# First head's K, V and q on GpSimd's queue, another order of the rooms of the second attention, and index sums over two score pieces

## The chip, the cores and the metric

The kernel runs on one core of a Trainium2 chip. The metric is the device time of one execution in microseconds. Engines are named as in the profile: PE is TensorE, DVE VectorE, ACT ScalarE, POOL GpSimd, SP SyncE. A `q` behind an engine's name (ACTq, SPq) marks what its instruction queue does without keeping the engine busy, the issue of a DMA above all.

## The reference

Two layers over 2048 tokens of width 1024 in float32. Layer 0 is a forgetting attention of 8 heads, layer 1 a sparse attention in which a light indexer picks at most 256 keys for each query. Cut to the lines that matter here:

```
for i in range(DEPTH):
    x = _layer_norm(DN_ALPHA * x + mixers[i % N_MIXERS](x), ln_g[i], ln_b[i], LN_EPS)
# layer 1, one block of 128 queries
isc = jnp.einsum('bqhd,bsd->bqhs', qi_b, ki) * di ** -0.5
isc = jnp.einsum('bqhs,bqh->bqs', jax.nn.relu(isc), wi_b)
isc = jnp.where(kpos <= qpos, isc, -jnp.inf)
_, idx = lax.top_k(isc, k_sel)
logits = jnp.einsum('bqhc,bqkc->bhqk', qf_b, sel) * dh ** -0.5
p = jax.nn.softmax(logits, axis=-1)
...
return (jax.nn.silu(gate) * o) @ w_out
```

So the index of a query block is a sum over 8 index heads of relu(score) times a weight. The kernel does not gather keys; it finds the threshold of the top 256, writes a mask, and runs a masked dense attention.

## The kernel before

Nearly every product is made of three float16 products (a high and a low half of each operand, `mm3`, lines 319 to 321), added in PSUM. PE has the most work of all engines. The program runs through these stages, with the times that they take in the profile: the projections of layer 0 (0 to 680 us), attention of layer 0 (680 to 1160), its output projection (1160 to 1430), the projections of layer 1 with the index woven in (1430 to 2030), attention of layer 1 (2030 to 2515), and its output projection (to the end).

**Rooms.** A stage takes its buffers from a pool. `PHASE` says how many rooms a tag has, `SIZE` how large they are, `ORDER` in which order the tags lie in the memory. The pools of successive stages lie over each other, so a tile of a new stage waits until the old tiles under it have been used for the last time (`reuse_waits="tile"`). For attention of layer 1 the old tiles are the eight `KV` (layer 1's input, two for each chunk of 512 tokens, used by the gate projection to its very end), and behind them the rooms of the index. `TURNED` names the rooms that transposed probabilities take in turn.

**Attention.** For each head `load_kv` loads K (two pieces, each in two DMAs in layer 1, `kr` and `kn`, line 994) and V (two pieces, line 1005); `load_chunk` loads the queries of a chunk (line 1013). Later heads' loads stand in SP's queue, head 0's K and V in ACT's. For a row of 128 queries PE makes the scores in pieces of 512 columns; DVE moves each to the row `PR` with bias or mask and takes the largest (line 1077, and 1090 scales it); ACT takes the exponential (1091) and copies it to float16 (`PP`, 1099); POOL subtracts to have the low half (`sub`, line 325); SP turns two rows by one transposing DMA (1104) into `PX`, `PT` or `PU`; PE multiplies by V (`O <- PX,V`).

**Index.** `scores` makes relu(q k) for each index head in pieces of at most 512 columns: two matmuls to a PSUM tile (1502, 1503), ACT's relu to a tile `SC` (1505, three rooms), and DVE's multiply and add to the row `x` in `GA`, `GB` or `GC` (1508 for the first head, 1510 for the others). The threshold search (`select`) is woven between, and so are the last projection tiles: `rest` in `dsa_jobs` goes tile by tile through 6 to 21, each over chunks 0 to 3. Tiles 14 to 21 are the gate, which is written to `scr_g` (372) and loaded again at `gate` (1029). Masks are made on DVE (1671) and stored from POOL's queue (1672).

**Order.** The code is written in one stream. A scheduler with its own timeline of costs (`schedule_with_timeline_sim`) then picks the order of the instructions of each engine, so any change of rooms or sizes can move instructions elsewhere. Each engine works through its own list in order. A DMA in SP's or ACT's list shares one of eight semaphores with other DMAs of these two and waits until the one before it on that semaphore has landed; DMAs of POOL's list have eight of their own. A waiting DMA holds up all that is behind it in the same list.

Of the kernel before, what the change touches and what calls it, by code (L numbers as in the profile page):

```python
# [15 lines left out]
F16 = mybir.dt.float16  # L16
OP = mybir.AluOpType
AF = mybir.ActivationFunctionType
# [29 lines left out]
BUFS = {"W": 6, "E": 8, "RW": 3, "QS": 2, "SC": 3, "ty": 9, "tz": 4, "tb": 2, "mb": 2}  # L48
PHASE = ({"KV": 8}, {"K": 4, "V": 2, "PT": 1, "PU": 1, "PX": 1, "PR": 4, "PP": 3, "I": 1, "N": 3},
         {"K": 4, "V": 2, "PT": 1, "PU": 1, "PX": 1, "PR": 4, "PP": 3, "M": 1, "N": 3}, {"P": 8},  # L50
         {"A": 3, "X": 15}, {"P": 8}, {})
ORDER = ((), ("N", "I", "PR", "PT", "pad1", "PU", "K", "PP", "V", "PX"),
         ("N", "M", "PX", "PR", "K", "V", "PP", "pad2", "PT", "PU"), ("pad3", "P"), ("A", "X"), (),
         ("st", "GB", "u", "GA", "GC", "spare"))
SIZE = {"K": 2048, "V": 4096, "PT": 8192, "PU": 8192, "PX": 8192, "PR": 4096, "PP": 4096, "I": 128, "N": 256,
        "M": 2432, "pad1": 3200, "pad2": 896, "pad3": 4096, "P": 4096, "A": 4096, "X": 4096, "st": 4096,
        "u": 3584, "spare": 4096, "GA": 8448, "GB": 10752, "GC": 7936}
TURNED = ("PT", "PU", "PX")

PS_BUFS = {"S": 3, "T": 2, "U": 2, "O": 1}  # L60
UTAGS = "SUSUS"
# [16 lines left out]
FTAGS = "STUSTUS"  # L78
SCAN = 2

WOP = (((0, 1), (2, 3), (4, 5), (6, 7)), ((3, 4), (2, 5), (6, 7), (1, 0)))
OGS = (0, 1, 2, 3), (0, 1, 1, 1)
OGE = 3
AHEAD = 13
# [146 lines left out]
class Trunk:  # L231
# [748 lines left out]
    def load_kv(self, layer, h):  # L980
        nc = self.nc
        st = {"layer": layer}

        rooms = FIRSTK[layer] if h == 0 else (("K", 1024), ("K", 1024))
        st["k"] = []

        def key(s):
            while sum(n for _, n in rooms[:len(st["k"])]) < s + 1024:
                tag, n = rooms[len(st["k"])]
                a = sum(n for _, n in rooms[:len(st["k"])])  # L990
                to = self.t(tag, [128, 2, n], F16)
                for rows, name, r in ((slice(0, 32), "kr", 0), (slice(32, 128), "kn", h * 96)) if layer else (
                        (slice(0, 128), "k1", h * 128),):
                    (nc.sync if h else nc.scalar).dma_start(
                        to[rows], self.scr[name][r:r + rows.stop - rows.start, :, a:a + n])
                st["k"].append(to)
                for b in range(a, a + n, 512):
                    st[b] = to[:, :, b - a:b - a + 512]

        def value(s):  # L1000
            if s == 0:
                st["v"] = self.t("V", [128, NT, 2, 128], F16)
            t = s // 128
            v = self.scr["v2" if layer else "v1"][h]
            (nc.sync if h else nc.scalar).dma_start(st["v"][:, t:t + 8], v[:, t:t + 8])

        return st, [partial(f, s) for f in (key, value) for s in range(0, S, 1024)]

    def load_chunk(self, layer, h, c):
        nc = self.nc  # L1010
        cs = {"layer": layer, "h": h, "c": c, "l": self.sums[:, c, 4 * h:4 * h + 4], "halves": []}
        q, parts = self.pair(("SC" if layer else "RW") if (h, c) == (0, ORD[layer][0]) else "E")
        nc.sync.dma_start(q, self.scr["q2" if layer else "q1"][c, h * 128:(h + 1) * 128])
        cs["q"] = parts
        if layer:
            return cs
        if self.rel[0] != h:
            self.rel = h, [self.t("W", [128, 1024]) for _ in range(2)]
            for a, t in enumerate(self.rel[1]):
                nc.sync.dma_start(t, self.scr["rel"][h:h + 1, a * 1024:a * 1024 + 1024].to_broadcast([128, 1024]))  # L1020
        cs["rel"] = self.rel[1]
        return cs
# [26 lines left out]
    def qk_tile(self, cs, j, i):  # L1049

        nc = self.nc
        c = cs["c"]
        qt = 4 * c + j
        n = (qt + 1) * 128
        at = i * (c + 1) * 512 if c < MERGE else 0
        if at == 0:
            cs["row"] = self.t("PR", [128, S])
            if c < MERGE or i:
                cs["pair"] = self.t("PP", [128, 2 * S], F16)
        off = 2 * i * (n - 128) if c < MERGE else 0  # L1060
        row = cs["row"][:, at:at + n]
        pair = cs["pair"][:, off:off + 2 * n] if c < MERGE or i else None
        mn = None
        for a, b in self.cuts(n, 512):
            w = b - a
            sc = self.psum(QTAGS[self.unit_i % len(QTAGS)])
            self.unit_i += 1
            qh, ql = (t[:, j * 128:(j + 1) * 128] for t in cs["q"])
            kh, kl = (cs["kv"][a][:, x, :w] for x in range(2))
            self.mm3(sc[:, :w], qh, ql, kh, kl, True, True)  # L1070
            if cs["layer"] == 0 and b == n:
                nc.tensor.matmul(sc[:, n - 128 - a:n - a], self.eye, self.cmask, start=False, stop=True,
                                 skip_group_check=True)
            for lo, bias in self.biases(cs, qt, a, b):
                hi = lo + bias.shape[-1]
                m2 = self.tiny(1)
                nc.vector.tensor_tensor_reduce(out=row[:, lo:hi], in0=sc[:, lo - a:hi - a], in1=bias,  # L1077
                                               op0=OP.add, op1=OP.min, scale=-1.0, scalar=3e38 if mn is None else mn,
                                               accum_out=m2)
                mn = m2  # L1080
            if b < n:
                yield
        if i == 0:
            yield "turn"
            self.half_i += 1
            turned = self.t(TURNED[self.half_i % len(TURNED)], [128, 4 * qt + 6, 128], F16)
            cs["halves"].append({"cs": cs, "half": j // 2, "T": turned})
        up = self.tiny(1)
        per, neg = (self.scale(x, cs["layer"]) for x in ("per", "neg"))
        nc.vector.tensor_scalar(up, mn, per, SHIFT * float(np.log(2.0)), op0=OP.mult, op1=OP.add)  # L1090
        nc.scalar.activation(row, row, AF.Exp, bias=up, scale=neg, accum_out=cs["l"][:, j:j + 1])  # L1091
        turned = cs["halves"][-1]["T"]
        if c >= MERGE and i == 0:
            self.turnq = [partial(self.turn_on_pe, row, turned, k, min(k + 4, qt + 1)) for k in range(0, qt + 1, 4)]
            yield
            return
        hi, lo = (pair.rearrange("p (k a q) -> p a k q", a=2, q=128)[:, x] for x in range(2))
        row = row.rearrange("p (k q) -> p k q", q=128)
        nc.scalar.activation(hi, row, AF.Copy)  # L1099
        self.sub(nc.gpsimd, lo, row, hi)  # L1100
        if c >= MERGE:
            turned = turned[:, 2 * qt:]
        if i:
            self.turns.append(nc.sync.dma_start_transpose(turned, cs["pair"][:, :turned.shape[1] * 128]))
        yield
# [184 lines left out]
    def dsa_jobs(self):  # L1290
# [157 lines left out]
        def over(tiles, *chunks):  # L1448
            return [(m, ch) for ch in chunks for m in tiles]
# [10 lines left out]
                ups.append((0.0, partial(at, ch + 1)))  # L1460
            ups += [(0.7, partial(up_value, ch, j, s)) for j in range(4) for s in range(2)]
        rest = []
        for m in range(6, 22):
            rest += jobs(over((m,), 0, 1, 2, 3))
        return first, second, weave(weave(rest, ups, *UPS), [(1.0, up)], UPL, UPL)


# [21 lines left out]
    def scores(self, qt, st, x):  # L1489
        nc = self.nc  # L1490
        n = (qt + 1) * 128
        self.stack(n)
        qs = self.t("QS", [128, 8, 128], F16)
        ready = nc.gpsimd.memset(x[:, n - 1:n], 0.0)
        load = nc.sync.dma_start(qs, self.scr["qis"].rearrange("(h p) t -> p h t", p=128)
                                 [:, :, qt * 128:(qt + 1) * 128])
        self.follow(load, ready, "no scores without a place for them")
        for h in range(H):
            for a, b in self.cuts(n):
                w = b - a  # L1500
                ps = self.unit()
                nc.tensor.matmul(ps[:, :w], qs[:, h], st[:, 0, a:b], start=True, stop=False)
                nc.tensor.matmul(ps[:, :w], qs[:, h], st[:, 1, a:b], start=False, stop=True)
                t = self.t("SC", [128, w])
                nc.scalar.activation(t, ps[:, :w], AF.Relu, scale=self.scales[:, 24:25])  # L1505
                w1 = self.wi[:, qt, h:h + 1]
                if h == 0:
                    nc.vector.tensor_scalar(x[:, a:b], t, w1, None, op0=OP.mult)
                else:
                    nc.vector.scalar_tensor_tensor(x[:, a:b], t, w1, x[:, a:b], op0=OP.mult, op1=OP.add)  # L1510

    def select(self, tiles, st):
        nc, V = self.nc, self.nc.vector
# [185 lines left out]
```

## Time and profile before

| | us |
|---|---|
| median of 3 runs | 2713.96 (2712.74 to 2714.54) |
| profiled execution | 2722.91 |
| its span | 2720.7 |
| PE busy in the span | 2503.0 (92%) |
| DVE busy | 1880.7 (69%) |
| ACT busy | 1416.8 (52%) |
| POOL busy | 857.6 (32%) |

The profiled execution is 8.95 us slower than the median and 2.2 us longer than its span. PE is busy nine tenths of the time, so what can be won without taking away matmuls is the rest, about 217 us, and it is spread over the stages unevenly. Shares of the whole span say little; the rows below are taken stage by stage.

### The profile page before, as it was taken

The page shows a single profiled execution, that of the slowest core. Times are in us where ns is not written, and L with a number is a line of the kernel's source. Part 1 is how long each engine was busy: PE and PEld are TensorE (multiplying, and loading weights), DVE is VectorE, ACT ScalarE, POOL GpSimd, SP SyncE. Part 2 cuts the span into 40 slices and gives each one's busy share as a digit, 9 for nine tenths or more (in the row PEclk, how much of TensorE's full clock was granted, in tenths as well). Part 3 has the DMA queues.
Part 4 walks back from the last instruction along what each step waited for, and adds up shares of the span by engine and source line. Part 5 has one row for each costly group of instructions (what it writes and reads, how often), then busy time and mean ns, then how long its engine had stood idle before and what let it go on. Part 6 is the DMA issues. An engine that isn't in the chain of part 4 may idle for free. (4 is left out here: it accounts for less than half of the span.)

```text
span 2720.7 us, 44075 instructions
## 1 busy us (share of the span) xinstructions
PE 2503.0 (92%) x15919; PEld 1634.1 (60%) x15919; DVE 1880.7 (69%) x4662; ACT 1416.8 (52%) x2283; POOL 857.6 (32%) x601
## 2 busy tenths in 40 slices
PE   8789999999888999899999989899996899998998
PEld 7688644444666666678845444344444666666787
DVE  4796656444666676667747899897975676776665
ACT  6463353321666676622326877774635666666210
POOL 2374653330333334432210211101003443344421
PEclk9899999999999999999999999999997999999999
DMA  7556745214989898864331432222568898877642
GB/s 253 167 188 202 239 127 178 78 67 129 223 192 204 191 211 179 170 195 138 126 99 50 127 97 58 78 70 85 175 210 197 186 198 197 192 175 168 188 143 88
DMA packets 583808, 424.19 MB, mean 156 GB/s; under 512 B 398048, under 2 KB 473584, under 8 KB 583584
## 3 DMA queue, kind: packets, MB, share of 16 engines
q1 hardware_dynamic: 580544, 412.78, 57.2%
q10 hardware_dynamic: 1984, 4.20, 0.6%
q0 software_dynamic: 1056, 4.36, 0.4%
q8 instruction: 125, 2.05, 0.3%
q14 instruction: 99, 0.81, 0.1%
HBM read 219.88 MB, written 109.08 MB: 121 GB/s over the span
## 5 line engine op out<-in xcount | busy, mean ns | idle before, releaser
L325 POOL TENSOR_TENSOR PP<-PR,PP 128x640 f16<-128x640 f32 (+3 forms) x192 | 375.1, 1971 | 659.0 <-ACT PP L1099 473.9
L1091 ACT ACTIVATE PR<-PR,ty,small 128x1152 f32<-128x1152 f32 (+15 forms) x256 | 329.6, 1288 | 198.5 <-DVE ty L1090 195.9
L325 POOL TENSOR_TENSOR W<-RW,W 128x512 fp32r<-128x512 f32 (+1 forms) x124 | 159.5, 1304 | 527.6 <-ACT W L328 459.6
L325 POOL TENSOR_TENSOR W<-A,W 128x512 f16<-128x512 f32 x114 | 136.4, 1215 | 223.2 <-ACT W L328 223.2
L320 PEld LDWEIGHTS <-W 128*128 128x128 f16 x1184 | 116.2, 98 | 140.0 <-issue 6.4
L321 PEld LDWEIGHTS <-W 128*128 128x128 f16 x1184 | 116.3, 98 | 137.6 <-issue 2.7
L319 PEld LDWEIGHTS <-W 128*128 128x128 f16 x1184 | 116.5, 98 | 136.9 <-issue 2.8
L1099 ACT ACTIVATE PP<-PR 128x640 f16<-128x640 f32 (+3 forms) x192 | 184.4, 977 | 24.8 <-DMA PX<-PP 14.5
L320 PE MATMUL T<-KV,W 128*128 128x512 f16 x464 | 177.0, 382 | 0.0
L319 PE MATMUL T<-KV,W 128*128 128x512 f16 x464 | 176.8, 381 | 0.1
L321 PE MATMUL T<-KV,W 128*128 128x512 f16 x464 | 176.7, 381 | 0.0
L328 ACT ACTIVATE W<-RW 128x512 fp32r<-128x512 f32 (+1 forms) x124 | 73.4, 628 | 184.7 <-PE U L320 92.7
L320 PEld LDWEIGHTS <-V 128*128 128x128 f16 x1152 | 116.2, 101 | 87.1 <-issue 64.0
L1077 DVE CUSTOM_DVE_ANT_0 PR<-S,W,ty 128x512 f32<-128x512 f32 (+3 forms) x209 | 138.9, 665 | 23.7 <-PE S L321 7.4
L319 PEld LDWEIGHTS <-V 128*128 128x128 f16 x1152 | 116.4, 101 | 62.8 <-DMA PU<-PP 10.7
L378 ACT ACTIVATE SC<-E,tz 128x512 f16<-128x512 f32 (+1 forms) x78 | 50.8, 682 | 170.8 <-DVE E L540 103.7
L319 PE MATMUL S<-K,E 128*128 128x512 f16 (+3 forms) x379 | 131.2, 347 | 1.3 <-DVE ty L1077 1.0
L320 PE MATMUL S<-K,E 128*128 128x512 f16 (+3 forms) x379 | 131.5, 347 | 0.0
L321 PE MATMUL S<-K,E 128*128 128x512 f16 (+3 forms) x379 | 131.1, 347 | 0.0
L1505 ACT ACTIVATE SC<-S,small 128x512 f32<-128x512 f32 (+2 forms) x182 | 111.7, 634 | 35.4 <-DVE GC L1510 7.1
L321 PEld LDWEIGHTS <-V 128*128 128x128 f16 x1152 | 116.4, 101 | 19.8
L1111 PE MATMUL T<-ident,PR 128*128 128x128 f32 x768 | 120.1, 277 | 3.8 <-DVE PX L325 2.1
(503 smaller groups left out, 7823.9 us busy)
## 6 DMA issues: line engine op xcount, KB each, us to landing
A<-in_fw SPq DMA_DIRECT2D x38, 512.0 KB
QS<-in_fw SPq DMA_DIRECT2D x32, 512.0 KB
E<-scr_g SPq DMA_DIRECT2D x64, 256.0 KB
scr_og<-SC SPq DMA_DIRECT2D x64, 256.0 KB
RW<-scr_og SPq DMA_DIRECT2D x64, 256.0 KB
E<-scr_q SPq DMA_DIRECT2D x62, 256.0 KB
V<-scr_v SPq DMA_DIRECT2D x28, 512.0 KB
scr_g<-E SPq DMA_DIRECT2D x48, 256.0 KB
```

The source lines that it names most:

```text
L319: first = mm(o, lh, rh, start=start, stop=False, skip_group_check=True)
L320: mm(o, lh, rl, start=False, stop=False, skip_group_check=True)
L321: mm(o, ll, rh, start=False, stop=stop, skip_group_check=True)
L325: eng.tensor_tensor(out=o, in0=a, in1=b, op=OP.subtract)
L328: self.nc.scalar.activation(hi, src, AF.Copy)
L378: nc.scalar.activation(out[0], src, AF.Copy, scale=scale)
L1077: nc.vector.tensor_tensor_reduce(out=row[:, lo:hi], in0=sc[:, lo - a:hi - a], in1=bias, op0=OP.add, op1=OP.min, scale=-1.0, scalar=3e38 if ...
L1091: nc.scalar.activation(row, row, AF.Exp, bias=up, scale=neg, accum_out=cs["l"][:, j:j + 1])
L1099: nc.scalar.activation(hi, row, AF.Copy)
L1111: nc.tensor.transpose(ps[:, (k - a) * 128:(k - a + 1) * 128], row[:, k * 128:(k + 1) * 128], self.ident)
L1505: nc.scalar.activation(t, ps[:, :w], AF.Relu, scale=self.scales[:, 24:25])
```

## The change

Three things. Head 0's K and V, and the first chunk's queries, are issued from POOL's queue in both layers. The rooms of attention of layer 1 lie in another order, its transposed tiles take their rooms in another turn, the output projection's weight rooms too (`WOP`), and the last four gate tiles go chunk by chunk (2, 3, 1, 0) instead of tile by tile. The index's relu writes two pieces side by side into one tile of 1024 columns (two rooms, the same tag that other stages use for `QS`), and DVE adds both in one instruction; the index queries move to a tag `qs` of their own.

```diff
-         {"A": 3, "X": 15}, {"P": 8}, {})
+         {"A": 3, "X": 15}, {"P": 8}, {"qs": 2})
-         ("N", "M", "PX", "PR", "K", "V", "PP", "pad2", "PT", "PU"), ("pad3", "P"), ("A", "X"), (),
-         ("st", "GB", "u", "GA", "GC", "spare"))
+         ("N", "PR", "K", "PX", "V", "PP", "PT", "PU", "M", "pad2"), ("pad3", "P"), ("A", "X"), (),
+         ("st", "GB", "u", "GA", "GC", "spare", "qs"))
-TURNED = ("PT", "PU", "PX")
+TURNED = ("PT", "PU", "PX"), ("PU", "PX", "PT")
-WOP = (((0, 1), (2, 3), (4, 5), (6, 7)), ((3, 4), (2, 5), (6, 7), (1, 0)))
+WOP = (((0, 1), (2, 3), (4, 5), (6, 7)), ((4, 3), (0, 1), (2, 5), (7, 6)))
@@ load_kv, key and value
-                    (nc.sync if h else nc.scalar).dma_start(
+                    (nc.sync if h else nc.gpsimd).dma_start(
-            (nc.sync if h else nc.scalar).dma_start(st["v"][:, t:t + 8], v[:, t:t + 8])
+            (nc.sync if h else nc.gpsimd).dma_start(st["v"][:, t:t + 8], v[:, t:t + 8])
@@ load_chunk
-        nc.sync.dma_start(q, self.scr["q2" if layer else "q1"][c, h * 128:(h + 1) * 128])
+        eng = nc.gpsimd if (h, c) == (0, ORD[layer][0]) else nc.sync
+        eng.dma_start(q, self.scr["q2" if layer else "q1"][c, h * 128:(h + 1) * 128])
@@ qk_tile
-            turned = self.t(TURNED[self.half_i % len(TURNED)], [128, 4 * qt + 6, 128], F16)
+            turned = self.t(TURNED[cs["layer"]][self.half_i % 3], [128, 4 * qt + 6, 128], F16)
@@ dsa_jobs
-        for m in range(6, 22):
+        for m in range(6, 18):
             rest += jobs(over((m,), 0, 1, 2, 3))
+        rest += jobs(over((18, 19, 20, 21), *ORD[0]))
@@ scores
-            for a, b in self.cuts(n):
-                w = b - a
-                ps = self.unit()
-                ...
-                t = self.t("SC", [128, w])
-                nc.scalar.activation(t, ps[:, :w], AF.Relu, scale=self.scales[:, 24:25])
+            cuts = self.cuts(n)
+            for i in range(0, len(cuts), 2):
+                two = cuts[i:i + 2]
+                lo, hi = two[0][0], two[-1][1]
+                t = self.t("QS", [128, hi - lo])
+                for a, b in two:
+                    ps = self.unit()[:, :b - a]
+                    ...
+                    nc.scalar.activation(t[:, a - lo:b - lo], ps, AF.Relu, scale=self.scales[:, 24:25])
-                    nc.vector.tensor_scalar(x[:, a:b], t, w1, None, op0=OP.mult)
+                    nc.vector.tensor_scalar(x[:, lo:hi], t, w1, None, op0=OP.mult)
-                    nc.vector.scalar_tensor_tensor(x[:, a:b], t, w1, x[:, a:b], op0=OP.mult, op1=OP.add)
+                    nc.vector.scalar_tensor_tensor(x[:, lo:hi], t, w1, x[:, lo:hi], op0=OP.mult, op1=OP.add)
```

**ACT, start of attention of layer 1.** The first row is the last gate tile's move out of PSUM; behind it stands, in the kernel before:

```order
L371 ACTIVATE E_23336<-O_23311,small 128x512
L1657 UNCONDITIONAL_BRANCH
L1005 DMA V_24193<-scr_v_69 128x2048
L994 DMA K_24213<-scr_kr 32x2x1024
L1091 ACT_TABLE_LOAD
L1091 ACTIVATE PR_24173,N_24152<-PR_24173,ty_24188,small 128x640
L994 DMA K_24213<-scr_kn 96x2x1024
L1005 DMA V_24193<-scr_v_69 128x2048
L1099 ACTIVATE PP_24174<-PR_24173 128x5x128
L1091 ACTIVATE PR_24173,N_24152<-PR_24173,ty_24207,small 128x768
```

and in the changed kernel, where line numbers from here on are one higher:

```order
L371 ACTIVATE E_23081<-O_23056,small 128x512
L1662 UNCONDITIONAL_BRANCH
L1092 ACT_TABLE_LOAD
L1092 ACTIVATE PR_23918,N_23897<-PR_23918,ty_23933,small 128x640
L1100 ACTIVATE PP_23919<-PR_23918 128x5x128
L1092 ACTIVATE PR_23918,N_23897<-PR_23918,ty_23952,small 128x768
L1100 ACTIVATE PP_23919<-PR_23918 128x6x128
L1092 ACTIVATE PR_23963,N_23897<-PR_23963,ty_23978,small 128x896
```

The four loads of V and K, which stood ahead of and between the first exponentials, are gone from ACT's list.

**POOL, the same place.** The last masks are stored, then the low halves of the first rows (`PP`) follow, in the kernel before:

```order
L1672 DMA scr_mask<-spare_16179 128x1664
L1672 DMA scr_mask<-spare_16179 128x1792
L1672 DMA scr_mask<-GA_19190 128x1920
L1672 DMA scr_mask<-GA_19190 128x2048
L325 TENSOR_TENSOR PP_24174<-PR_24173,PP_24174 128x5x128
L325 TENSOR_TENSOR PP_24174<-PR_24173,PP_24174 128x6x128
L325 TENSOR_TENSOR PP_24219<-PR_24218,PP_24219 128x7x128
```

and now (line 1677 is 1672 of before):

```order
L1677 DMA scr_mask<-spare_16116 128x1664
L1677 DMA scr_mask<-spare_16116 128x1792
L1677 DMA scr_mask<-GA_19063 128x1920
L1677 DMA scr_mask<-GA_19063 128x2048
L1005 DMA V_23938<-scr_v_69 128x2048
L994 DMA K_23958<-scr_kr 32x2x1024
L994 DMA K_23958<-scr_kn 96x2x1024
L1005 DMA V_23938<-scr_v_69 128x2048
L325 TENSOR_TENSOR PP_23919<-PR_23918,PP_23919 128x5x128
L325 TENSOR_TENSOR PP_23919<-PR_23918,PP_23919 128x6x128
```

The loads stand behind the last mask and ahead of the first low half.

**DVE, the index, the first row of 1536 columns.** `GB` is the row of index sums, `flog` holds the index's weights; `SC` and `QS` are the relus. In the kernel before:

```order
L1508 TENSOR_SCALAR GB_16472<-SC_16495,flog 128x512
L1510 SCALAR_TENSOR_TENSOR GB_16472<-SC_16501,flog,GB_16472 128x512
L1510 SCALAR_TENSOR_TENSOR GB_16472<-SC_16507,flog,GB_16472 128x512
L1315 TENSOR_SCALAR flog<-T_16325 128x32
L1510 SCALAR_TENSOR_TENSOR GB_16472<-SC_16513,flog,GB_16472 128x512
L1272 SCALAR_TENSOR_TENSOR E_16282<-T_16284,small,E_16282 128x512
L1273 SCALAR_TENSOR_TENSOR T_16284<-T_16284,small,E_16280 128x512
L1510 SCALAR_TENSOR_TENSOR GB_16472<-SC_16519,flog,GB_16472 128x512
```

and in the changed kernel (1513 and 1515 are 1508 and 1510 of before):

```order
L1513 TENSOR_SCALAR GB_16409<-QS_16417,flog 128x1024
L1624 COPY_PREDICATED sv_14921<-sv_14921 128x3
L1513 TENSOR_SCALAR GB_16409<-QS_16427,flog 128x512
L1515 SCALAR_TENSOR_TENSOR GB_16409<-QS_16433,flog,GB_16409 128x1024
L1515 SCALAR_TENSOR_TENSOR GB_16409<-QS_16443,flog,GB_16409 128x512
L1591 SCALAR_TENSOR_TENSOR sv_14921<-sv_14921,ztab 128x3
```

Three pieces of 512 columns have become one of 1024 and one of 512. Over the program 304 such instructions become 176, with as many columns in all; the matmuls and relus are as many as before.

**The first row of scores.** Its `PR` room lay over tiles of chunks 0 and 1, of which the last gate tile used chunk 3; now it lies over tiles of chunks 2 and 0, and chunk 0 is the last that the gate uses. Head 0's first K room lay over chunk 3's tiles and now lies over those of chunks 1 and 3. So K's room comes free before the last gate tiles, and the first row waits for the last one.

## Rows read from the trace of the kernel before

**Rows 1.** Page, part 1: busy time of each engine and its share.
```profile
PE 2503.0 (92%) x15919; PEld 1634.1 (60%) x15919; DVE 1880.7 (69%) x4662; ACT 1416.8 (52%) x2283; POOL 857.6 (32%) x601
```

**Rows 2.** Windows by stage: length, busy of PE, PEld, DVE, ACT, POOL, PEclk, DMA share, GB/s.
```profile
1430.00:1850.00 420.00, 388.33 (x1845) 182.34 (x1844) 370.23 (x1081) 314.07 (x570) 61.88 (x54) 0.98 0.29 80
...
2030.00:2110.00 80.00, 53.10 (x341) 35.20 (x339) 40.12 (x128) 43.49 (x67) 24.61 (x13) 0.81 0.89 205
2110.00:2510.00 400.00, 362.31 (x2716) 263.71 (x2714) 282.64 (x862) 264.76 (x396) 162.69 (x85) 0.98 0.84 186
```

**Rows 3.** Waits of PE, 2026 to 2075: what for, us in total, times, longest.
```profile
PE U L319 <- DMA K<-scr_kn: 11.3, 1, 11.3
PE O L319 <- DMA PX<-PP: 6.2, 1, 6.2
PE S L319 <- DVE ty L1077: 3.3, 1, 3.3
```

**Rows 4.** Timeline of ACT, 2028 to 2052: start, us, instruction, [idle before <-releaser].
```profile
2027.83 0.69 ACT L371 ACTIVATE E<-O,small 128x512 f32<-128x512 f32 x1 [4.49 <-PE O L321]
...
2035.64 1.28 ACT L1091 ACT_TABLE_LOAD   x1 [7.12 <-DMA E<-scr_g]
...
2039.32 0.57 ACTq L994 DMA_DIRECT2D K<-scr_kn  x1
2041.30 0.34 ACTq L1005 DMA_DIRECT2D V<-scr_v  x1
2041.69 0.74 ACT L1099 ACTIVATE PP<-PR 128x640 f16<-128x640 f32 x1 [3.74 <-DMA E<-scr_g]
```

**Rows 5.** Timeline of DVE, 2020 to 2060.
```profile
2021.71 0.67 DVE L1077 CUSTOM_DVE_ANT_0 PR<-U,QS 128x512 f32<-128x512 f32 x1
...
2037.98 0.29 DVE L1077 CUSTOM_DVE_ANT_0 PR<-S,cmaskb 128x128 f32<-128x128 f32 x1 [4.58 <-ACT PR L1091]
```

**Rows 6.** Timeline of POOL, 2015 to 2064.
```profile
2022.09 0.54 POOL L1672 DMA_DIRECT2D scr_mask<-GA  x1 [0.17 <-issue]
2042.51 1.39 POOL L325 TENSOR_TENSOR PP<-PR,PP 128x640 f16<-128x640 f32 x1 [19.88 <-ACT PP L1099]
2045.36 1.64 POOL L325 TENSOR_TENSOR PP<-PR,PP 128x768 f16<-128x768 f32 x1 [1.46 <-ACT PP L1099]
```

**Rows 7.** Timeline of SP, 2026 to 2064.
```profile
2050.43 7.89 SPq L1104 DMA_TRANSPOSE PX<-PP  x1
2058.49 4.64 SPq L1104 DMA_TRANSPOSE PT<-PP  x1
```

**Rows 8.** Timeline of PE, 2030 to 2062.
```profile
2060.58 0.37 PE L319 MATMUL O<-PX,V 128*128 128x256 f16 x1 [6.19 <-DMA PX<-PP]
```

**Rows 9.** Windows at the start of attention of layer 1.
```profile
2050.50:2060.60 10.10, 3.91 (x14) 1.97 (x15) 1.00 (x3) 0.90 (x5) 2.76 (x3) 0.50 1.18 195
2060.60:2069.60 9.00, 8.27 (x41) 5.72 (x42) 0.00 (x0) 0.99 (x2) 2.02 (x2) 0.50 1.03 261
```

**Rows 10.** Waits of PE in the index, 1430 to 1850.
```profile
PE S L1502 <- ACT SC L1505: 18.6, 18, 3.1
PE U L1502 <- ACT SC L1505: 11.8, 12, 2.9
```

**Rows 11.** Groups of DVE, kept apart by shape: count, busy us, mean ns, idle before.
```profile
L1510 DVE SCALAR_TENSOR_TENSOR GA<-SC,flog,GA 128x512 f32<-128x512 f32 x70 | 53.3, 777 | 13.6 <-ACT SC L1505 12.9
...
L1634 DVE SCALAR_TENSOR_TENSOR spare<-GA,sv,small 128x1024 bf16<-128x1024 f32 x1 | 1.3, 1283 | 0.0
```

**Rows 12.** Page, part 5: ACT's relu in the index.
```profile
L1505 ACT ACTIVATE SC<-S,small 128x512 f32<-128x512 f32 (+2 forms) x182 | 111.7, 634 | 35.4 <-DVE GC L1510 7.1
```

**Rows 13.** Timeline of ACT, 670 to 690, start of attention of layer 0.
```profile
675.81 0.33 ACTq L1005 DMA_DIRECT2D V<-scr_v  x1
682.05 0.72 ACT L378 ACTIVATE SC<-E,tz 128x512 f16<-128x512 f32 x1 [6.28 <-DMA scr_k<-SC]
```

**Rows 14.** Timeline of PE, 676 to 700.
```profile
684.34 0.59 PE L319 MATMUL S<-QS,RW 128*128 128x512 f16 x1 [3.99 <-DVE ty L1077]
```

## What the change should do to the time, predicted before it ran

> **What bounds the kernel now.** Read the page's busy shares first: PE works 92% of the span [rows 1], so a change that takes no matmul away can win only PE's idle time. The windows by stage come second, because that idle time is not spread evenly: of the 80 us at the start of attention of layer 1 PE is busy 53.1, so it idles 26.9; of the 420 us of the index 31.7; of the 400 us of attention that follow 37.7 [rows 2]. The reader is to see that the first of these loses a third of its time. Third, PE's waits say what ends its idle time. At the start of attention it waits 11.3 us for K, 6.2 for the first transposed probabilities and 3.3 for DVE, 20.8 in all [rows 3]. In the index it waits 18.6 + 11.8 = 30.4 us for ACT's relu to free a PSUM tile [rows 10], and ACT in its turn waits for DVE's sums to free an `SC` room: that is what the page names behind the relu [rows 12].
>
> Fourth, ACT's timeline shows why the start is slow. ACT has the last gate tile moved by 2028.5 (2027.83 + 0.69), then sits 7.12 us before its table load and later 3.74 before the first copy to `PP`, both released by a DMA [rows 4]. No data is missing there: the loads of V and K stand in ACT's own list, ahead of the exponential or among them, and each waits until an older DMA on its semaphore has landed. DVE is 4.58 us late behind that [rows 5], and POOL's first low half comes 19.88 us after its list was last busy [rows 6].
>
> **Part 1: head 0's loads leave ACT's list.** It removes four DMA issues and the 7.12 + 3.74 = 10.9 us of stops [rows 4]. Step by step, with the gate's end where it was: the last move ends at 2028.5, the table load (1.28) at 2029.8, so the first exponential starts there and no longer at 2036.9. The first row's `PR` room is now free only at the last gate tile, so DVE starts that row at about 2027.8 instead of 2021.71; two pieces of at most 0.67 us [rows 5] are done by 2029.2, under the table load. That new wait costs nothing as long as ACT loads its table; without that cover it would cost 1.4 us. Behind it in DVE's list stand the next rows' pieces, which need scores that PE makes only then. The second low half ended at 2045.36 + 1.64 = 2047.0 [rows 6]; 10.9 us earlier is 2036.1. The transposition that needs it was issued at 2050.43 [rows 7], held a little longer by the K load, and the first product with V came at 2060.58 [rows 8], 10.15 us after that issue. With the issue at 2036.1 the product comes at 2046.3, 14.3 us earlier. PE's wait for K goes as well, as that load is issued early.
>
> What is late next is this transposition, and the one behind it at 2058.49 [rows 7]. The ends: 20.8 us would be all of PE's waits [rows 3]; 0 if the loads in SP's list, which stand ahead of the transposition, take as long as before, for the DMA engines are full there (share 1.18 and 1.03, [rows 9]). Four loads have moved ahead of the gate's end into time with room, so I take 12, near to the 14.3.
>
> POOL's list now holds the loads between the last mask and the first low half. An issue takes about 0.54 us there [rows 6], so four take 2.2 us, against 19.88 us in which POOL had nothing to do: no cost.
>
> **The clock.** [...] PE will still idle some 9 us (20.8 less 12) before the transposed tile is there, so the clock probably falls again: I take 2, with 0 and 6 as ends.
>
> **Part 2: the rooms, the turn, the gate's order, `WOP`.** No instruction is added. Their worth is that K and V can be issued before the gate's end, which is counted above; later rows keep their depth of rooms. I add 0. The ends are 3 us either way, by the third of the waits at the start, 3.3 for DVE [rows 3].
>
> **Part 3: attention of layer 0.** There ACT issues a V load at 675.81 and then waits 6.28 us until a store of K's has landed [rows 13]; PE idles 3.99 [rows 14]. With V loaded earlier the store shares the DMA engines with less. Ends 0 and 4, I take 2.
>
> **Part 4: the index sums.** 128 of DVE's 304 sums go, with no column fewer. A sum over 512 columns takes 777 ns; the one DVE operation of 1024 float32 columns in the trace with a weight for each row takes 1283 [rows 11]. So a pair saves up to 2 x 777 - 1283 = 271 ns, or 35 us in all. From the other side: at 1283 / 1024 = 1.25 ns a column, 512 columns cost 641 ns, which leaves 136 ns fixed for each instruction, or 17 us. I take the middle, 26 us: DVE then works 344 of the 420 us instead of 370 [rows 2]. Not all comes back to PE: its 30.4 us of waits go only where DVE was the slowest, and DVE also runs the threshold search. I take 12, with 0 and 30 as ends. The relus (634 ns each, [rows 12]) stay, and two rooms of two pieces hold four pieces instead of three.
>
> [...]
>
> **The sum.** 12 + 2 + 0 + 2 + 12 = 28 us. The profiled execution took 2722.91 us for a span of 2720.7, so it should come to 2695; the median, 8.95 lower, to 2713.96 - 28 = 2686.
>
> **The rivals.**
>
> A. The loads are late from POOL. V and K stand behind the last mask stores, which need DVE's last masks; POOL may be slow to issue them while DVE is busy. Then K lands no sooner than before, and the 14 us of part 1 and the clock are gone: 28 - 14 = 14, 2700. For it: the last mask was issued only at 2022.09, 5.7 us before the gate's end. Against it: that issue took 0.54 us right behind DVE's mask [rows 6], and K had until 2050 before. [...] No row here shows a load issued from POOL, so this rests on the mask stores alone.
>
> B. The index gives nothing, since PE, ACT and DVE wait for one another in a ring and the search decides: 28 - 12 = 16, 2698. For it: DVE's work was 370 of 420 us, PE's 388 [rows 2], so both are near their limits and a shorter DVE leaves PE's own.
>
> C. Slower: the pair is too coarse. A room now comes free only after a sum of 1283 ns instead of 777, and the sum can't begin before a second relu of 634. If each of PE's 30 waits [rows 10] grew by 1283 - 777 + 634 = 1140 ns, the index would lose 34 us; less 16 from the other parts that is 18 slower, 2732. It decides once a wait grows by more than 16 / 30 = 0.53 us. Against it: four pieces fit where three did, and PE has other tiles between.
>
> D. The waits only change their names: attention at DMA share 0.84 [rows 2] takes back what the start gains, and the index is as B. 2713.
>
> **Chances.** The forecast 0.50, A 0.14, B 0.17, C 0.11, D 0.08. A, B and the forecast are faster by over 0.2% (5.4 us, about what a measurement can tell from no change): 0.81. Within it 0.08, slower 0.11. The forecast's own range is 2674 to 2698, from its middle terms halved or half as large again. The range to hold 8 in 10 goes from 2666 (20.8 + 2 + 20 of the index and 5 more of the clock and of layer 0) to 2714, which leaves C out and the far end of the index.
>
> **What would show it.** In ACT's timeline of the changed kernel no idle time released by a DMA between the last gate tile and the first `PP`; POOL's first low half about 4 us behind the gate's end instead of 15; the first product with V about 18 us behind it instead of 33; PE's wait for K gone, and its wait for the first transposed tile longer or equal. In the index DVE's busy time near 344 us, a sum over 1024 columns between 1250 and 1420 ns, PE's wait for ACT's relu below 20 us. I am wrong if ACT still waits for a DMA at that place, if the transposition is issued no earlier than 20 us behind the gate's end, or if PE's wait in the index stays at 30 us or grows.

## The result and the profile after

The changed kernel takes 2693.24 us (median of 4 runs, 2690.03 to 2698.6), the kernel before 2714.25 beside it: a ratio of 0.9928, interval 0.991 to 0.9946. That is 21 us faster; 28 were forecast. The forecast was 2686, with 2674 to 2698 as its own range and 2666 to 2714 to hold 8 in 10, so the time lies in both. Timed again beside the experiments the ratio came to 0.992 (0.9899 to 0.9941). Single runs of one kernel differ by 10 us and more, so parts of the change are read from stages of the profiles, each of one execution. The two profiles of the changed kernel agree to 2.2 us in every stage.

A stage here begins and ends with an instruction that all versions have, by its start in PE's timeline: **start**, up to the first score of attention of layer 0; **A0**, from there to its first product with V; **index**, from the first index product to the last gate product (its start is called the gate's end); **A1**, from there to the first product with V of layer 1; **rest**, from there to the last such product. Each ratio is against the kernel before as timed beside that version (2714 to 2718 us).

| us | median of runs, ratio | start | A0 | index | A1 | rest |
|---|---|---|---|---|---|---|
| before | 2714.25 | 673.0 | 29.6 | 607.0 | 33.2 | 467.7 |
| changed | 2693.24, 0.9928 | 680.4 | 26.4 | 594.6 | 26.0 | 465.1 |
| changed, again | 2693.70, 0.992 | 679.0 | 26.5 | 594.3 | 27.0 | 462.9 |
| pairs only | 2707.41, 0.997 | 679.7 | 28.8 | 596.1 | 31.6 | 467.7 |
| queues and rooms | 2704.74, 0.9958 | 675.1 | 26.6 | 606.4 | 26.1 | 467.1 |
| queues only | 2703.29, 0.9962 | 674.4 | 26.3 | 605.4 | 27.0 | 465.8 |
| rooms only | 2713.35, 0.999 | 676.7 | 30.5 | 607.1 | 28.6 | 464.7 |
| five single rooms | 2709.86, 0.9983 | 671.3 | 30.0 | 601.0 | 30.5 | 463.5 |
| pair rooms, two sums | 2716.10, 0.9999 | 670.9 | 30.9 | 602.5 | 34.3 | 462.0 |
| next head later | 2684.63, 0.9891 | 674.8 | 27.9 | 595.0 | 16.1 | 467.6 |
| ... and gates later | 2700.09, 0.9949 | 672.2 | 27.0 | 593.9 | 13.2 | 486.3 |
| ... gates on POOL | 2695.27, 0.9911 | 675.0 | 26.2 | 594.3 | 23.7 | 472.5 |

So 12.4 us come from the index, 7.2 from A1, 3.2 from A0, 2.6 from the rest and 2.2 from the last stage (182.8 to 180.6, by the last product with V and PE's last instruction). Another 3.5 come from the part between A0 and the index, which the table leaves out, and 7.4 are lost in the start: in all the two profiles differ by 23.9. The 7.4 us are hardly the change's: the pairs alone, whose queues there are those of before, show 679.7, and over all versions the start goes from 670.9 to 680.4 without regard to the queues.

The table also shows how far a stage scatters without an edit that touches it. A1 is 30.5 to 34.3 us in the four versions with the loads on ACT and the old rooms of attention, and 26.0 to 27.0 in the four with the loads on POOL and nothing moved in SP's list. The kernel before lies in the upper half of the first group; by the means of the two groups the gain is 5.9 us and not 7.2.

**ACT at the start of attention of layer 1.** ACT's timeline of the changed kernel (start, us, instruction, [idle before]):

```profile
2016.17 0.69 ACT L371 ACTIVATE E<-O,small 128x512 f32<-128x512 f32 x1 [4.44 <-PE O L321]
2016.87 1.28 ACT L1092 ACT_TABLE_LOAD   x1
2018.17 0.92 ACT L1092 ACTIVATE PR<-PR,ty,small 128x640 f32<-128x640 f32 x1
...
2019.21 0.74 ACT L1100 ACTIVATE PP<-PR 128x640 f16<-128x640 f32 x1
```

Where [rows 4] had 7.12 and 3.74 us of idle time, nothing stands in brackets behind the last gate tile's move. The exponential begins 2.0 us after that move's start; before it was 9.1 (2036.94 behind 2027.83).

**POOL** in the same stretch issues the loads and has the first two low halves early:

```profile
2009.80 0.53 POOL L1005 DMA_DIRECT2D V<-scr_v  x1 [0.33 <-DMA scr_g<-E]
2010.33 0.56 POOL L994 DMA_DIRECT2D K<-scr_kr  x1
2010.88 0.66 POOL L994 DMA_DIRECT2D K<-scr_kn  x1
2011.54 0.57 POOL L1005 DMA_DIRECT2D V<-scr_v  x1
2020.04 1.39 POOL L325 TENSOR_TENSOR PP<-PR,PP 128x640 f16<-128x640 f32 x1 [7.93 <-ACT PP L1100]
2021.91 1.65 POOL L325 TENSOR_TENSOR PP<-PR,PP 128x768 f16<-128x768 f32 x1 [0.49 <-ACT PP L1100]
```

The four issues take 0.53 to 0.66 us each and end 3.6 us ahead of the gate's end, 2015.75. The first low half comes 4.3 us behind it; before it was 15.1 [rows 6].

**SP** is where the gain stops:

```profile
2016.88 0.32 SPq L372 DMA_DIRECT2D scr_g<-E  x1
...
2018.25 0.38 SPq L1014 DMA_DIRECT2D E<-scr_q  x1
2021.02 0.32 SPq L1030 DMA_DIRECT2D E<-scr_g  x1
...
2024.62 0.32 SPq L1030 DMA_DIRECT2D E<-scr_g  x1
2025.04 0.38 SPq L1005 DMA_DIRECT2D V<-scr_v  x1
...
2029.44 0.59 SPq L994 DMA_DIRECT2D K<-scr_kn  x1
2031.18 8.27 SPq L1105 DMA_TRANSPOSE PT<-PP  x1
2039.55 4.63 SPq L1105 DMA_TRANSPOSE PU<-PP  x1
```

The second low half ended at 2023.56, but the transposition was issued at 2031.18, 15.4 us behind the gate's end (23.1 before, [rows 7]), and its issue took 8.27 us. Behind the gate's end 15 issues stand ahead of it: the last gate tile's store, six loads of queries and gate, and eight loads of head 1, one behind the other to 2030.0. Issued without a stop they last 7.3 us. Two of the gate's loads wait besides (the gaps from 2018.6 to 2021.0 and from 2021.8 to 2024.6, 5.2 us together), until a store of the gate has landed.

**PE's waits** in that stretch, 2014 to 2063 (what for, total, times, longest):

```profile
PE O L319 <- DMA PT<-PP: 8.1, 1, 8.1
PE U L319 <- DMA E<-scr_q: 2.8, 1, 2.8
PE U L319 <- DVE ty L1078: 2.0, 1, 2.0
```

The 11.3 us for K are gone [rows 3]; the wait for the first transposed tile has grown from 6.2 to 8.1. The clock still fell. Windows in which it was granted at 0.50 in this profile (length, busy PE, PEld, DVE, ACT, POOL, PEclk, DMA share, GB/s):

```profile
2024.60:2027.80 3.20, 2.86 (x7) 1.04 (x8) 0.27 (x3) 3.20 (x10) 1.30 (x1) 0.50 0.97 274
2031.40:2044.90 13.50, 5.36 (x24) 2.94 (x23) 0.99 (x3) 1.09 (x3) 2.69 (x3) 0.50 1.14 234
2051.90:2055.10 3.20, 3.20 (x10) 1.28 (x9) 2.91 (x12) 1.67 (x1) 0.00 (x0) 0.50 1.07 348
```

and in the second profile of the changed kernel:

```profile
2021.80:2031.80 10.00, 7.37 (x22) 3.11 (x22) 4.08 (x14) 5.47 (x14) 5.06 (x4) 0.50 0.98 266
2035.40:2048.90 13.50, 6.89 (x34) 4.78 (x35) 0.00 (x0) 1.04 (x2) 2.02 (x2) 0.50 1.09 244
```

PE was busy 11.4 us at the lower level in the first and 14.3 in the second, against 12.2 in the kernel before [rows 9]: the clock gave nothing back.

**The index.** The sums (count, busy us, mean ns, idle before) and PE's waits for the relu:

```profile
L1515 DVE SCALAR_TENSOR_TENSOR GB<-QS,flog,GB 128x1024 f32<-128x1024 f32 x21 | 27.8, 1324 | 3.4 <-ACT QS L1510 3.2
...
L1515 DVE SCALAR_TENSOR_TENSOR GA<-QS,flog,GA 128x1024 f32<-128x1024 f32 x21 | 26.9, 1282 | 11.6 <-ACT QS L1510 11.3
```

```profile
PE S L1508 <- ACT QS L1510: 15.5, 13, 3.6
PE U L1508 <- ACT QS L1510: 6.6, 5, 2.3
```

1282 to 1324 ns for 1024 columns, where [rows 11] had 1283 for another operation; the waits are 22.1 us instead of 30.4 [rows 10]. The whole index stage as a window, before and changed:

```profile
1420.40:2027.40 607.00, 571.85 (x2687) 265.04 (x2686) 534.13 (x1439) 404.10 (x702) 70.52 (x66) 0.99 0.34 101
```

```profile
1421.20:2015.80 594.60, 569.08 (x2687) 264.68 (x2686) 510.53 (x1306) 404.10 (x702) 77.64 (x75) 0.99 0.35 102
```

DVE works 23.6 us less; PE idles (length less busy) 25.5 us instead of 35.2.

**Layer 0.** ACT's wait for the store and PE's gap behind it, changed kernel:

```profile
686.75 0.72 ACT L378 ACTIVATE SC<-E,tz 128x512 f16<-128x512 f32 x1 [3.52 <-DMA scr_k<-SC]
```

```profile
689.04 0.38 PE L319 MATMUL S<-QS,RW 128*128 128x512 f16 x1 [1.23 <-DVE ty L1078]
```

6.28 us have become 3.52, and 3.99 have become 1.23 [rows 13, 14].

### The profile page after: what moved, and what is told of

Its sections match the earlier page's. It is cut to its first block, busy times and chain, and to the rows that moved or that the text cites. A ratio compares the mean times of both kernels' runs of the same rounds, so it can differ in the third digit from the quotient of the medians.

```text
span 2696.8 us, 43822 instructions
## 1 busy us (share of the span) xinstructions
PE 2491.6 (92%) x15919; PEld 1627.9 (60%) x15919; DVE 1864.8 (69%) x4534; ACT 1417.0 (53%) x2283; POOL 865.9 (32%) x615
## 5 line engine op out<-in xcount | busy, mean ns | idle before, releaser
L1100 ACT ACTIVATE PP<-PR 128x640 f16<-128x640 f32 (+3 forms) x192 | 184.4, 977 | 22.4 <-DMA PT<-PP 12.2
L328 ACT ACTIVATE W<-RW 128x512 fp32r<-128x512 f32 (+1 forms) x124 | 73.4, 628 | 180.4 <-PE U L320 86.9
L1078 DVE CUSTOM_DVE_ANT_0 PR<-S,W,ty 128x512 f32<-128x512 f32 (+3 forms) x209 | 138.9, 665 | 26.1 <-PE S L321 10.3
L1510 ACT ACTIVATE QS<-S,small 128x512 f32<-128x512 f32 (+2 forms) x182 | 112.1, 635 | 35.8 <-DVE GB L1515 10.3
```

What stands on the lines that cost most here:

```text
L328: self.nc.scalar.activation(hi, src, AF.Copy)
L1510: nc.scalar.activation(t[:, a - lo:b - lo], ps, AF.Relu, scale=self.scales[:, 24:25])
```

## The experiments

**Pairs only**, from the kernel before: the diff's lines in `scores` and the tag `qs`.

> Only the index sums over two pieces (with the qs tag); queues and rooms as before. Theory 1 (DVE's fixed cost per sum is what the index lost, part 4 of the prediction): 12 us faster (2702), the whole of it won between the first index matmul and the last gate tile, PE's wait for ACT's relu falls from 30 to about 22 us; the start of attention of layer 1 unchanged, first product with V still 33 us behind the gate's end. Rival (the gain between index and gate's end comes from the new order of the gate tiles or the freed queues): less than 4 us faster.

0.997 (0.9956 to 0.9985), 8 us faster by the medians; index 596.1. The gain sits where theory 1 put it, and neither the queues nor the rooms of attention are needed for it. How much of the 10.9 us of the stage is the edit's is taken up below, with the two runs on the relu's rooms.

**Queues and rooms**, without `scores`:

> Head 0's loads on POOL and the new rooms, without the pairs. Theory 1: about 9 us faster (2705): first product with V 26 us behind the gate's end instead of 33, the index as before (30 us of waits for the relu). Rival: if the pairs brought nothing, all 21 us faster (2693).

0.9958 (0.9942 to 0.9975), 10 us. A1 is 26.1, the index 606.4. With the pairs' 8 this makes 18 of the 21; the intervals of the two are wider than the 3 that are missing.

**Queues only**:

```diff
-                    (nc.sync if h else nc.scalar).dma_start(
+                    (nc.sync if h else nc.gpsimd).dma_start(
```

(and the same for V and the first queries).

> Head 0's loads on POOL, rooms and gate order as before. Theory 1 (ACT's stops for its loads were the loss; the rooms matter little, since the first transposition waits behind 16 loads in SP's list whatever the rooms are): 7 to 9 us faster (2706), the same 26 us from the gate's end to the first product with V. Rival (the rooms decide, since K's room is free only at the last gate tile and POOL would then block its low halves): no more than 3 us faster, POOL idle before a load.

0.9962 (0.9947 to 0.9976): as with the rooms. A1 27.0 against 26.1: the queues carry this part. POOL's timeline:

```profile
2015.85 0.56 POOL L994 DMA_DIRECT2D K<-scr_kr  x1 [2.02 <-PE O L321]
...
2022.10 1.40 POOL L325 TENSOR_TENSOR PP<-PR,PP 128x640 f16<-128x640 f32 x1 [4.41 <-DVE ty L1091]
```

POOL did stop at K's room, for 2.0 us, as the rival said. But the stop ends 1.9 us ahead of the gate's end (2017.77), and the first low half comes 4.3 us behind it, as in the changed kernel.

**Rooms only**: `ORDER`, `TURNED`, `WOP` and the gate's order.

> New rooms, turn and gate order; head 0's loads stay in ACT's and SP's lists. Theory 1: within 3 us of before (2713), as ACT still stops for the semaphores of its loads. Rival (rooms decide): 6 us or more faster, ACT's stops gone.

0.999 (0.9975 to 1.0004), no measurable change of the whole. But A1 is 28.6, which is 4.6 below before and 1.9 below the lowest of the four versions with the old rooms; theory 1 did not expect that. ACT's timeline of it:

```profile
2034.35 1.28 ACT L1091 ACT_TABLE_LOAD   x1 [8.06 <-DMA E<-scr_g]
2035.19 0.57 ACTq L994 DMA_DIRECT2D K<-scr_kn  x1
...
2036.98 0.74 ACT L1099 ACTIVATE PP<-PR 128x640 f16<-128x640 f32 x1 [0.32 <-ACT PR L1091]
```

The first stop is even longer, 8.06, but the second is 0.32 instead of 3.74, as K's second load follows 1.4 us behind its first (4.3 before). That need not be the new rooms' doing: with five single rooms, below, where attention has the old rooms, the stops are 10.03 and 0.17:

```profile
2024.04 0.74 ACT L1099 ACTIVATE PP<-PR 128x640 f16<-128x640 f32 x1 [0.17 <-ACT PR L1091]
```

The two stops together are 8.4 us here and 10.2 to 12.5 in the four profiles with the old rooms. So the rooms may give 2 us or so of what the queues win; one profile does not settle it, and the two do not add (26.1 with both, 27.0 with queues alone).

**The changed kernel again**:

> The changed kernel once more, beside the three that follow. Median 2693 plus or minus 4. If the 7 us that its first profile lost before attention of layer 0 were the run's and not the change's, attention starts anywhere between 673 and 680 us this time; if they were the change's (head 0's K loads among POOL's weight halves), at 680 again. First product with V 26 us behind the gate's end.

Median and A1 as expected. The start came at 679.0 once more, which by itself speaks for neither; it was read from the other versions, above.

**Next head later.** In `load_kv` of the changed kernel:

```diff
+                    if layer and h == 1:
+                        self.follow(load, self.turns[1], ...)
```

(for K's loads and V's).

> The changed kernel, with head 1's K and V loads of layer 1 told to stand behind the first two transpositions in SP's list (eight issues that stood ahead of them). Theory 1 (what ended the start after the change is SP's list: 16 loads of 0.4 to 0.65 us and their waits ahead of the transposition, which then shares full DMA engines with them): transposition issued 9 to 10 us behind the gate's end instead of 15, first product with V 18 to 20 us instead of 26, 5 to 7 us faster than the changed kernel (2687). Rival (the low halves on POOL or the DMA engines set it, not the list): the issue stays at 15 us or the transposition takes longer by as much, within 2 us of the changed kernel.

SP's timeline:

```profile
2012.88 0.47 SPq L1018 DMA_DIRECT2D E<-scr_q  x1
2017.17 0.32 SPq L1034 DMA_DIRECT2D E<-scr_g  x1
2017.67 4.21 SPq L1109 DMA_TRANSPOSE PT<-PP  x1
...
2022.61 4.56 SPq L1109 DMA_TRANSPOSE PU<-PP  x1
```

The gate's end is 2007.78, so the transposition is issued 9.9 us behind it, and it takes 4.21 us instead of 8.27 without the eight loads issued just ahead of it. A1 is 16.1: better than the 18 to 20 expected. 2684.63, ratio 0.9891 (0.9867 to 0.9914): faster than the changed kernel (0.992) by 9 us in the medians of the same chip, five of its six runs below the fastest of that kernel, and the fastest version here. SP's list was what ended the start.

**... and gates later**: the same line behind head 0's gate loads.

> As the one before, and head 0's four gate loads of layer 1 also behind the first two transpositions; the queries of later chunks then fall behind them too, as they take rooms in turn with the gates. Theory 1: the transposition no longer waits for the last gate store either and is issued 8 us behind the gate's end, first product with V after 16 to 18 us; but PE's scores of the second chunk wait for their queries, 3 us or more, so no faster than the one before, perhaps slower. Rival: another 2 us or more faster.

A1 is 13.2, but only since 35 matmuls stand ahead of the first product with V instead of 50; PE idles 5.6 us in it, against 4.7 with the next head alone. The rest takes 486.3. PE's waits, from the gate's end on for 110 us:

```profile
PE U L319 <- DMA E<-scr_q: 14.0, 2, 11.5
```

The queries take rooms of `E` in turn with the gates and fell behind the masks and K in SP's list; 11.5 of the 14.0 us fall into the rest stage, which is 19 us longer than with the next head alone. PE idles 59.4 us in that stage instead of 48.8. The other 8 us are the clock's: PE was busy 31.5 us of the stage at a granted clock of 0.50, against 15.9, and at the full level that work takes half (matmuls of 512 columns start 0.22 us apart there instead of 0.43, below). In all 0.9949 (0.9928 to 0.9971), slower than with the next head alone.

**Five single rooms**, from the kernel before: relus take tags SC, SC, QS, SC, QS in turn, one sum for each.

> The kernel before, with single sums over 512 columns as there, but five rooms for the relus instead of three (the two QS rooms beside the three of SC; index queries in a tag of their own). 304 sums, DVE's work as before. Theory 1 (the pairs win by taking DVE's fixed cost away): index to gate's end 604 to 607 us as before, at most 3 us faster (2712). Rival (they win because four pieces can be in flight instead of three): 594 to 598 us, 8 to 12 us faster, as the pairs.

601.0: between the 604 to 607 of theory 1 and the 594 to 598 of the rival. **Pair rooms, two sums**, from the pairs alone:

```diff
-                    nc.vector.scalar_tensor_tensor(x[:, lo:hi], t, w1, x[:, lo:hi], op0=OP.mult, op1=OP.add)
+                for a, b in two:
+                    o, y = x[:, a:b], t[:, a - lo:b - lo]
+                    nc.vector.scalar_tensor_tensor(o, y, w1, o, op0=OP.mult, op1=OP.add)
```

> As the pairs alone, but with two sums of 512 columns for each pair of relus instead of one of 1024: the rooms of the pairs (two tiles, four pieces) without the spared DVE instructions. From the index's first product to the gate's end the kernel before takes 606 us, the pairs 595, five single rooms 601. Theory 1 (DVE's fixed cost): 604 us or more, as the rooms come free later than single ones. Rival (rooms in flight): 595 to 599, as the pairs. A middle near 600 would say that both count by half.

602.5, between theory 1 and the rival again. The index stage of both as windows, single rooms first:

```profile
1409.40:2010.40 601.00, 566.78 (x2686) 263.70 (x2685) 532.81 (x1437) 403.74 (x702) 70.71 (x66) 0.99 0.34 100
```

```profile
1414.10:2016.60 602.50, 570.41 (x2683) 264.87 (x2682) 533.00 (x1432) 404.08 (x702) 66.76 (x63) 0.99 0.34 98
```

PE's waits for the relu, with pair rooms and two sums:

```profile
PE S L1506 <- ACT QS L1508: 14.5, 11, 4.9
PE U L1506 <- ACT QS L1508: 6.7, 7, 2.9
```

DVE works 533 us in both, as before (534.1), and yet the stage is 4 to 6 us shorter. What PE idles in it tells the two apart: 35.2 us before, 36.1 with queues and rooms, 34.2 with five single rooms, 32.1 with pair rooms and two sums, 29.0 with the pairs alone and 25.5 and 27.1 in the two profiles of the changed kernel. The other part of the difference is PE's busy time for the same matmuls, 566.8 us with five rooms and 571.9 before, and it is the clock's. Windows of the index stage in which the granted clock was 0.50, four of the kernel before and then two with five single rooms:

```profile
1469.00:1472.20 3.20, 3.02 (x8) 1.08 (x8) 3.12 (x6) 2.07 (x5) 1.40 (x1) 0.50 0.63 158
1510.00:1516.60 6.60, 5.89 (x15) 2.26 (x15) 5.09 (x12) 6.55 (x12) 0.27 (x1) 0.50 0.14 50
1585.00:1588.20 3.20, 3.02 (x9) 1.13 (x8) 3.10 (x8) 2.57 (x5) 1.23 (x1) 0.50 0.46 133
1919.50:1922.70 3.20, 3.20 (x9) 1.21 (x8) 2.99 (x17) 1.35 (x3) 0.00 (x0) 0.50 1.00 328
```

```profile
1694.70:1697.90 3.20, 3.20 (x10) 1.21 (x9) 3.20 (x8) 2.83 (x6) 0.00 (x0) 0.50 0.07 11
1773.20:1776.40 3.20, 2.67 (x8) 1.13 (x8) 2.55 (x11) 3.20 (x6) 0.00 (x0) 0.50 0.00 0
```

PE was busy 15.1 us in the first four and 5.9 in the last two. At the full level that work takes half (matmuls of 512 columns start 0.43 us apart at 0.50 and 0.22 apart at the full clock), so 4.6 of the 5.0 us are explained. In all twelve profiles PE's busy time in this stage goes from 566.5 to 571.9 us; less half of what it did at the lower clock it is 562.5 to 563.9. The two profiles of the changed kernel have 12.6 and 6.5 us of such work in this stage, so it goes with the single execution and not with the edit. The length of the stage is therefore no measure of an edit here; the idle time is.

By idle time the pair rooms give 3.0 us (35.2 to 32.1) and the spared instructions another 3.1 (32.1 to 29.0), about half each; as two profiles of one kernel differ by 1.6, neither share is exact. PE's waits for the relu fall with the rooms alone, from 30.4 us [rows 10] to 21.2, and are 22.7 with the pairs alone. The medians give more to the spared instructions: five single rooms come to 0.9983 (0.9966 to 1.0) and pair rooms with two sums to 0.9999 (0.9988 to 1.001), no measurable change, the pairs to 0.997.

**... gates on POOL**, from the kernel with the next head later: `eng = nc.gpsimd if layer and h == 0 else nc.sync` for the gate's load.

> The kernel with head 1's loads behind the first transpositions, and head 0's four gate loads of layer 1 issued by POOL as well: SP's list then holds four query loads ahead of the transposition and none that shares a semaphore with the gate's last store. Theory 1: transposition 7 to 8 us behind the gate's end, first product with V after 13 to 15 us instead of 16, and no wait of PE for later queries beyond 5 us: 2 to 3 us faster than head 1's loads alone (2682). Rival (POOL then stops for a room of the gates ahead of its low halves): POOL's first low half later than 4 us behind the gate's end, same or slower.

The rival. POOL's timeline:

```profile
2008.59 0.55 POOL L1682 DMA_DIRECT2D scr_mask<-spare  x1
2014.51 0.54 POOL L1035 DMA_DIRECT2D E<-scr_g  x1 [5.38 <-ACT PP L1105]
...
2017.17 0.56 POOL L994 DMA_DIRECT2D K<-scr_kr  x1
...
2018.97 3.00 POOL L325 TENSOR_TENSOR PP<-PR,PP 128x640 f16<-128x640 f32 x2
```

POOL stood 5.38 us at a gate load, with the masks and V and K behind it. K was loaded after the gate's end (2008.21), PE waited 12.1 us for it, and the first low half came 10.8 us behind the gate's end: 23.7 us instead of 16.1. The ratio is 0.9911 (0.989 to 0.9932) against 0.9891, whose intervals overlap, so it is A1 that shows the loss.

## Why the prediction was nearly right

28 us were forecast and 21 measured. Part 1 is 4.8 short and the clock 2, which is the order of what is missing; the other parts came close, one of them by luck.

**Part 1, 12 us forecast, 7.2 measured** (5.9 by the means above). The removed stops were right to the microsecond: first exponential, first low half and the wait for K came as written. The step that was mis-sized is the transposition's issue, forecast 8.7 us behind the gate's end (2036.1 against 2027.37) and found at 15.4; the first product with V then came 26.0 us behind the gate's end and not about 18. The prediction named SP's loads as the low end of this term and then took the high one, on the ground that four loads had moved away; it did not count the 15 issues that stay ahead of the transposition behind the gate's end. At 0.3 to 0.65 us each they last 7.3 us without any wait, and 5.2 us of waits come on top. Eight of them moved away gave 10 us back (A1 from 26.0 to 16.1).

**The clock, 2 forecast.** Nothing came. The 2 was the author's estimate and no run shows it: PE was busy 11.4 and 14.3 us at a granted clock of 0.50 in the two profiles of the changed kernel and 12.2 before [rows 9]; at the full clock that work takes half (0.22 us a matmul of 512 columns instead of 0.43, above), so 6 us were the most to win by this estimate. The prediction let the clock gain from shorter waits; PE still stood 8.1 us before the first transposed tile and 2.8 for queries, and the clock fell again, as the prediction itself held probable.

**Part 2, 0 forecast.** Right for the sum, inside the ends given. Rooms alone show an A1 that is 1.9 us below the lowest with the old ones, but with the queues they give only 0.9. The last stage takes 180.4 to 181.5 us in all seven profiles with the new rooms and 182.1 to 182.8 in the five without, so they give about 1.5 us there, which the prediction did not see.

**Part 3, 2 forecast.** 3.2 measured: A0 is 26.2 to 27.0 with the loads on POOL, but for one version (27.9), and 28.8 to 30.9 with them on ACT. The reason given, that the store shares the DMA engines with less, was not tested.

**Part 4, 12 forecast, 12.4 measured.** DVE's work fell by 23.6 us over the stage, forecast 26, between the ends of 17 and 35. In the window from 1430 to 1850 alone DVE is busy 361 us and not 344, since more of the program falls into it (PE has 1898 instructions there instead of 1845). That the time agrees to half a microsecond is luck: PE idles 9.6 us less in the first profile and 8.0 in the second, and the rest, 2.8 and 4.6, is busy time, of which the windows at the lower clock account for 1.3 and 4.3. So 8 to 10 us are the change's. The prediction gave all of it to the spared instructions; by idle time, half of what the pairs alone win is the rooms', by the medians hardly any. PE's wait for the relu came to 22.1 us and not below 20.

**The rivals.** A did not come: POOL's loads were issued 4 us ahead of the gate's end and PE never waited for K. Its mechanism, one list in order, came in the last experiment, where it cost 7.6 us of A1. POOL was not slow to issue the loads, 0.53 to 0.66 us each; but DVE stood idle from 2008.64 to 2016.17 in that profile, over all four issues, so what a busy DVE does to them was not shown. B fell with the pairs alone, C with PE's waits of 22.1 us, and D with both.

## What to carry to other kernels

When a stop in one engine's list is taken away, count what stands in the next list that the work passes, issue by issue, before taking the gain whole; here SP's list kept 7 of the 14 us that were expected. A load that shares a list with work on the path should stand behind the first piece of that work, and one told to do so gave about as much as the queue change itself (9 us against 10), as long as no tile that PE needs soon falls behind with it. Parts that are each a few microseconds in runs that scatter by ten are read from stages between fixed instructions of the profile, and in a stage from PE's idle time: here its busy time in the index changed by 5 us with the clock that the single execution was granted.

## What was not expected of the hardware

A transposing DMA of the same size took 8.27 us with eight loads issued just ahead of it and 4.21 without them; with the eight moved away but POOL's loads issued late, in the last experiment, it took 7.28. PE's busy time for the same matmuls of the index differs by 5 us between single executions, as the clock was granted at 0.50 for more or less of it. The run's own scatter lies mostly in the first stage, 670.9 to 680.4 us with the same instructions of PE. And one operation of 1024 columns, 1282 to 1324 ns, spares DVE 23.6 us of busy time in 128 instructions, 184 ns each. The durations of the index's sums, added up, fall by 30.7 us (206.4 to 175.7), 240 ns each; the busy time falls by less, as the durations of neighbours overlap in it, by 87.6 us over all of DVE's work in the index stage before and by 78.6 in the changed kernel.
